# A decoder trunk on one core: sums copied into a second PSUM bank so that later matmuls accumulate onto the copy

## The chip, the core and the metric

The kernel runs on one core of one Trainium2 chip. The metric is the device time of one execution in microseconds (us); lower is better. TensorE (PE in the profile) multiplies, ScalarE (ACT) and VectorE (DVE) read its results out of PSUM, GpSimd (POOL) adds weights in SBUF, and SyncE's queue (SP) issues most of the transfers.

## The reference, cut to what matters

```python
def reference(x, ...):                       # x: 1 x 1024 positions x 1024 channels, fp32
    h = x
    for layer in range(2):
        y = _rms_norm(h, mix_norm_g[layer])
        if layer == 0: y = _chunk_gating_mixer(y, ...)       # u * (W_s v + b), then w_out
        else:          y = _dilated_attention_mixer(y, ...)  # 3 groups, dilation 1, 4, 16
        h = h + y
        y = _rms_norm(h, mlp_norm_g[layer])
        h = h + jnp.square(jax.nn.relu(y @ w_up[layer])) @ w_down[layer]   # 1024 -> 4096 -> 1024
    return _rms_norm(h, final_norm_g)
```

The attention projects q, k and v (3 groups of 8 heads of 64 channels each), adds to the scores a bias looked up in a table of 32 buckets, and merges the groups by their softmax denominators.

## The kernel before

**Split numbers.** Every fp32 factor is split into a high part that the matmul unit takes exactly (type fp32r) and a low rest: ACT makes the high part with a copy, DVE the rest with a subtraction. The helper `split` (profile lines L211 and L212) records both, so these two lines stand for all splits of the program and a reader goes by the tile: `wp` and `whi` are weights, `hx` hidden values of the MLP, `tr` other operands. A product of two factors is three matmuls (high x high, high x low, low x high), all recorded at L183.

**Seven products.** Up projection, down projection and q/k projections use Strassen's scheme in Winograd's form. A tile of 256 x 1024 outputs is made of seven products in place of eight; each product is 128 x 512 outputs over four blocks of 128 inputs, so 4 x 3 = 12 matmuls into one PSUM bank of 128 x 512. The seven results are then summed in four ways: c11 = 1 + 2, c12 = 1 + 6 + 5 + 3, c21 = 1 + 6 + 7 + 4 and c22 = 1 + 6 + 5 + 7 (numbers are products). The banks come from two pools, named `mm` (3 banks) and `at`.

**Up projection** (loop `for q in range(2, 16)`, L785 on, in each of two layers; a "tile" below is one turn of it). Product 1 goes to a bank `a`, 5 to `d`, 6 to `b`, 7 to `e`, and then 2, 3 and 4 accumulate in `a`, `d` and `e`. ACT copies `a` to `u` and `d` to `c22` (L796, L808); DVE makes five additions of 128 x 512: `u += b` (L819), `c22 += e` (L826), `c22 += u` (L834), `c12 = u + d` (L845) and `c21 = u + e` (L850). ReLU and squaring follow on ACT (L733, L734). `hidden_terms` forms the differences that the down projection needs and stores them as `hid`.

**Weights of a tile** are loaded one tile ahead (`r`), summed by POOL (L354 to L359) and split in the order of a generator, `Weights.steps`, which `more()` pumps once after each product. In layer 0, `coming_late` meanwhile loads weights of layer 1 (`t<-in_w_up`), splits them (`tr`) and stores them (`wlup`); three of its steps follow each tile. `late` loads them back.

**Down projection** (`Down`): products into `mm` and `at` banks, `b` and `h` updated by DVE (L940, L952, L921). While it ends, `begin_attention` issues the loads and splits of the first value weights.

**Attention.** `unit_qk` makes q and k of one pair of heads in one group, as seven products again: one ACT copy (L1208) and five DVE additions (`total`, L1200), then q and k are split with a strided order (`halves`, L1194 and L1195). The next unit's products are interleaved on PE with scores (L1268 on DVE, exponentials L1270 on ACT), transposes (L190) and value products of the unit before. `prepare` makes the q/k weights of coming units ahead of time (list `PREPARED`); its additions are L485 and its loads `r<-in_w_qkv`. `bias_rows` looks the bias table `tab` up by three fp32 matmuls with one-hot rows.

**What sets the order.** Each engine runs its own queue in order. The queues follow the order of the code, except that instructions under `tc.high_priority(offset=PRIO)` move up to 60 places ahead, and that side work comes from generators which are advanced by an estimated PE clock (`flow`, with the paces in `PACE` and `LAT`). `tc.issue_after(x)` puts what is in it behind x.

## Time and profile before

| | before |
|---|---|
| time, median of 3 runs | 2146.59 us (2145.32 to 2150.58) |
| the profiled execution's own time | 2148.0 us |
| its span in the profile | 2146.3 us (1.7 us lie around it) |
| granted TensorE clock, mean | 0.996 |
| PE busy / DVE / ACT / POOL | 2111.2 / 1629.2 / 1116.2 / 521.4 us |
| matmuls | 10192 |

A row of a timeline gives start, duration, engine, line, operation, what is written from what, and in brackets how long the engine had been idle before it and what it waited for. A row of groups gives busy time and mean nanoseconds of one. Matmul rows end later than the next one starts, since matmuls are pipelined: the distance of their starts is what counts.

### The profile page before, as it was taken

The numbers are of one execution on the slowest core, as the hardware profiler recorded it, in microseconds if no ns is written. First come the engines' busy times: TensorE is split into PE (matmuls) and PEld (weight loads), VectorE is DVE, ScalarE is ACT, GpSimd is POOL, SyncE is SP. The second block draws the span as 40 slices with busy tenths as digits, with TensorE's granted clock in tenths as the row PEclk, the third lists the DMA queues.
The fourth block names the chain that finished last, engine by engine and source line by source line (L and its number), as shares of the span: only waits on it lengthen the run. The fifth ranks groups of instructions, "written<-read, shape, count | busy, mean of one in ns | idle before, by whom it ended". The sixth has DMA issues, their size and how long they took to land.

```text
span 2146.3 us, 30685 instructions
## 1 busy us (share of the span) xinstructions
PE 2111.2 (98%) x10192; PEld 1740.0 (81%) x10192; DVE 1629.2 (76%) x2998; ACT 1116.2 (52%) x2258; POOL 521.4 (24%) x381
## 2 busy tenths in 40 slices
PE   9999999999999999999999999999999999999997
PEld 7888887888888888788877788877788888788886
DVE  7877678777889777788367777768876667987776
ACT  7645446555564444345256665655555556544432
POOL 2000124333333332420200000001433332432244
PEclk9999999999999999999999999999999999999999
DMA  6326814566655443449797646481154443654432
GB/s 217 124 75 217 275 69 164 172 214 213 217 184 169 162 157 119 132 161 335 268 288 219 175 153 186 162 275 69 57 198 151 152 162 121 204 168 143 143 108 79
DMA packets 214962, 367.68 MB, mean 171 GB/s; under 512 B 38809, under 2 KB 66580, under 8 KB 214804
## 3 DMA queue, kind: packets, MB, share of 16 engines
q1 hardware_dynamic: 205664, 364.37, 51.2%
q10 hardware_dynamic: 9140, 1.36, 0.4%
q8 instruction: 80, 1.31, 0.2%
q14 instruction: 78, 0.64, 0.1%
HBM read 239.13 MB, written 126.52 MB: 170 GB/s over the span
## 4 chain that ended last, share of the span: by engine, by line
PE 80%; DVE 10%; ACT 4%; DMA 4%; issue 2%; SPq 0%; POOL 0%; ACTq 0%; DVEq 0%; POOLq 0%
PE at L183 43%; PE mm L183 36%; PE at L190 1%; DVE tr L212 1%; DVE h L311 1%; DMA r<-in_w_v 1%; DMA V<-vd 1%; DVE h L921 1%; DVE y L212 1%; DVE wp L212 1%; ACT t L1270 1%; DVE N L1309 1%; DMA wd<-tr 1%; DVE t L1437 0%; ACT q L1194 0%
## 5 line engine op out<-in xcount | busy, mean ns | idle before, releaser
L211 ACT ACTIVATE wp<-r 128x512 fp32r<-128x512 f32 (+2 forms) x411 | 244.0, 597 | 346.1 <-PE at L183 222.0
L183 PE MATMUL at<-hx,wp 128*128 128x512 f32 x1740 | 406.3, 389 | 2.2 <-DVE h L921 2.0
L183 PEld LDWEIGHTS at<-hx,wp 128*128 128x128 f32 x1740 | 326.3, 188 | 71.6 <-DVE h L921 2.8
L212 DVE TENSOR_TENSOR wp<-r,wp 128x512 fp32r<-128x512 f32 (+2 forms) x404 | 308.9, 770 | 67.9 <-ACT wp L211 64.5
L183 PE MATMUL mm<-y,wp 128*128 128x512 f32 x1344 | 338.9, 395 | 1.9 <-issue 1.1
L183 PE MATMUL at<-t,wp 128*128 128x512 f32 x1344 | 313.7, 389 | 0.0
L183 PEld LDWEIGHTS at<-t,wp 128*128 128x128 f32 x1344 | 252.3, 188 | 52.4
L183 PEld LDWEIGHTS mm<-y,wp 128*128 128x128 f32 x1344 | 248.4, 188 | 54.5 <-issue 2.2
L267 POOL TENSOR_TENSOR t<-t 128x512 f32<-128x512 f32 (+1 forms) x64 | 81.6, 1275 | 703.6 <-ACT t L262 546.8
L354 POOL TENSOR_TENSOR t<-r 128x512 f32<-128x512 f32 (+3 forms) x62 | 88.7, 1431 | 582.5 <-DMA r<-in_w_dn 275.9
L183 PE MATMUL mm<-hx,wp 128*128 128x512 f32 x696 | 169.6, 390 | 0.7 <-DVE hx L212 0.3
L183 PE MATMUL mm<-y,whi 128*128 128x512 f32 x512 | 158.3, 390 | 0.0
L212 DVE TENSOR_TENSOR hx<-t,hx 128x512 fp32r<-128x512 f32 x192 | 148.7, 782 | 11.6 <-ACT hx L211 11.5
L183 PEld LDWEIGHTS mm<-hx,wp 128*128 128x128 f32 x696 | 130.2, 188 | 29.6 <-issue 1.0
L183 PE MATMUL mm<-t,wp 128*128 128x512 f32 x576 | 154.1, 403 | 0.0
L211 ACT ACTIVATE hx<-t 128x512 fp32r<-128x512 f32 x192 | 118.7, 627 | 44.2 <-DMA t<-hid 39.3
L921 DVE TENSOR_TENSOR h<-h,at 128x512 f32<-128x512 f32 x144 | 98.0, 681 | 54.6 <-PE at L183 53.9
L183 PEld LDWEIGHTS mm<-t,wp 128*128 128x128 f32 x576 | 102.6, 188 | 21.4
L183 PE MATMUL at<-y,wp 128*128 128x512 f32 x480 | 118.7, 390 | 0.0
L183 PEld LDWEIGHTS mm<-y,whi 128*128 128x128 f32 x512 | 95.6, 188 | 19.5
L1270 ACT ACTIVATE t<-t,st 128x128 f32<-128x128 f32 (+1 forms) x192 | 84.4, 441 | 50.7 <-DVE st L1268 49.4
L183 PEld LDWEIGHTS at<-y,wp 128*128 128x128 f32 x480 | 89.9, 188 | 19.9 <-issue 1.3
(214 smaller groups left out, 3531.9 us busy)
## 6 DMA issues: line engine op xcount, KB each, us to landing
t<-hid SPq DMA_DIRECT2D x182, 256.0 KB, 4.6
wd<-tr SPq DMA_DIRECT2D x154, 256.0 KB, 3.2
wp<-wd SPq DMA_DIRECT2D x77, 512.0 KB, 4.6
hid<-t SPq DMA_DIRECT2D x140, 256.0 KB, 2.7
r<-in_w_up SPq DMA_DIRECT2D x120, 256.0 KB, 2.7
r<-in_w_dn SPq DMA_DIRECT2D x80, 256.0 KB, 2.6
hid<-b SPq DMA_DIRECT2D x56, 256.0 KB, 2.9
r<-in_w_v SPq DMA_DIRECT2D x48, 256.0 KB, 3.7
```

What stands on the lines that cost most here:

```text
L183: nc.tensor.matmul(out, lhsT, rhs, **kw)
L190: nc.tensor.transpose(out, src, ident)
L211: nc.scalar.activation(hi, src, AF.Copy)
L212: (engine or nc.vector).tensor_tensor(lo, src, hi.bitcast(F32), op=ALU.subtract)
L267: nc.gpsimd.tensor_tensor(self.acc, self.acc, sq, op=ALU.add)
L311: nc.vector.tensor_tensor(x, x, ps, op=ALU.add)
L354: tt(r3, r[0, 0], r[1, 0], op=ALU.subtract)
L921: return engine.tensor_tensor(hs[i, s], hs[i, s], src, op=ALU.add).ins
L1270: nc.scalar.activation(p[:, c], p[:, c], AF.Exp, bias=m, scale=-1.0, accum_out=dn)
L1309: nc.vector.tensor_tensor(o, o, pv[r, c], op=ALU.add)
```

## The change

For tiles q = 5 to 15 of the up projection, ACT copies product 1 from its bank into a second bank `sums`, and products 6, 7 and 4 accumulate there. Between them ACT copies 1 + 6 out to `c12`, and DVE adds 1 + 6 + 7 to `c22`; the bank ends as c21. Two DVE additions are left (`c22 += sums`, L885; `c12 += d`, L891). The products run in the order 1, 5, 6, 2, 7, 3, 4, as against 1, 5, 6, 7, 2, 3, 4. The old form stays for q = 2 to 4 as `opening`. `unit_qk` is changed in the same way: three ACT copies, two additions, the last half of k straight from the bank, and the order 1, 5, 6, 2, 7, 3, 4 in place of 1, 6, 5, 2, 7, 3, 4.

Further edits: the order in which a tile's weights are split; `coming_late` takes its steps after the second, fourth and sixth call of `more` within a tile; the value weights are issued behind the last product-4 addition of the down projection; `prepare` waits at least 8000 ns of the estimated clock after its loads where these go to `raw` buffers (the last list of `PREPARED`); `bias_rows` uses two fp32r matmuls on a split table in place of one fp32 matmul; layer 1's first weights come back in another order.

```diff
@@ Weights.steps
-            for p, src in ((5, r[1, 0]), (7, r3), (6, r[1, 1]), (2, r[0, 1]), (3, r[0, 0])):
+            for p, src in ((5, r[1, 0]), (6, r[1, 1]), (2, r[0, 1]), (7, r3), (3, r[0, 0])):
@@ prepare
-            yield pace
+            yield max(pace, 8000.0) if own is raw else pace
@@ mlp, up projection
+            def more():
+                forward()
+                calls[0] += 1
+                if layer == 0 and q >= OPEN and calls[0] in LATER:
                     next(coming_late, None)
...
+            if q < OPEN:
+                c11, c21, c12, c22 = opening(q, w, more)
+            else:
+                a = at_bank()
+                product(a, w[1], x.t[1])
+                more()
+                sums = mm_bank()
+                with tc.high_priority(offset=PRIO):
+                    nc.scalar.activation(sums, a, AF.Copy)
...
+                d = at_bank()
+                product(d, w[5], x.t[5])
+                more()
+                c22 = temp()
+                nc.scalar.activation(c22, d, AF.Copy)
...
+                product(sums, w[6], x.t[6], True)
+                more()
+                c12 = temp()
+                with tc.high_priority(offset=PRIO):
+                    nc.scalar.activation(c12, sums, AF.Copy)
...
+                product(a, w[2], x.t[2], True)
+                more()
+                c11 = temp()
+                squared(c11, a)
+                product(sums, w[7], x.t[7], True)
+                more()
+                nc.vector.tensor_tensor(c22, c22, sums, op=ALU.add)
+                squared(c22)
...
+                product(d, w[3], x.t[3], True)
+                more()
+                nc.vector.tensor_tensor(c12, c12, d, op=ALU.add)
+                squared(c12)
+                product(sums, w[4], x.t[4], True)
+                c21 = temp()
+                squared(c21, sums)
@@ bias_rows
+            oh = rtemp()
+            nc.scalar.activation(oh[0:33, 0:VEC], raw[0:33, 0:VEC], AF.Copy)
             ps = at_bank()
-            matmul(ps[0:8, 0:VEC], tab[:, 8 * g:8 * g + 8], oh[0:33, 0:VEC], passes=4, start=True, stop=True)
+            for e, t in enumerate(tabs):
+                matmul(ps[0:8, 0:VEC], t[:, 8 * g:8 * g + 8], oh[0:33, 0:VEC], start=e == 0, stop=e == 1)
@@ begin_attention
-            firsts.extend(value_weights(0))
+            with tc.issue_after(emptied):
+                firsts.extend(value_weights(0))
@@ unit_qk
-        c = temp()
-        with tc.high_priority(offset=PRIO):
-            nc.scalar.activation(c, a, AF.Copy)
-        b = mm_bank()
-        product(b, w[6], x[6])
-        more()
-        total(c, b, c)
+        sums = copied(mm_bank(), a)
         d = mm_bank()
         product(d, w[5], x[5])
         more()
-        k1 = total(c, d)
+        k1 = copied(temp(), d)
+        product(sums, w[6], x[6], True)
+        more()
+        q1 = copied(temp(), sums)
         product(a, w[2], x[2], True)
...
-        halves(1, 1, own(total(k1, e, k1), g))
+        halves(1, 1, own(total(k1, sums, k1), g))
         product(d, w[3], x[3], True)
         more()
-        halves(0, 1, own(total(c, d), g))
-        product(e, w[4], x[4], True)
+        halves(0, 1, own(total(q1, d, q1), g))
+        product(sums, w[4], x[4], True)
         more()
-        halves(1, 0, own(total(c, e), g))
+        halves(1, 0, own(sums, g))
@@ before layer 1's up projection
+    first, order = [{}, {}], [(q, i, j) for j in range(2) for q in range(2) for i in range(2)]
+    for q, i, j in order[:6]:
+        first[q][i, j] = late("up", q, i, j)
```

Three places show how the queues move. The first is ACT's queue in layer 0's up projection at the start of tile q = 7, before: `mm_4531` is product 1, `at_4550` product 5, `t_4486` a layer-1 weight that `coming_late` loaded.

```order
L211 ACTIVATE wp_4544<-r_4520 128x512 [waits DMAHW3_49,PE_49]
L211 ACTIVATE tr_4488<-t_4486 128x512 [waits DMAHW7_49]
L796 ACTIVATE t_4548<-mm_4531 128x512 [waits DMAHW6_49]
L808 ACTIVATE t_4566<-at_4550 128x512 [waits PE_49]
L211 ACTIVATE wp_4563<-r_4516 128x512 [waits Pool_49]
```

The same place after the change: `at_4531` is product 1, `mm_4550` the bank of the sums, `at_4552` product 5, `t_4548` the layer-1 weight.

```order
L862 ACTIVATE mm_4550<-at_4531 128x512 [waits PE_49]
L213 ACTIVATE wp_4544<-r_4520 128x512 [waits DMAHW0_49]
L213 ACTIVATE wp_4565<-r_4516 128x512 [waits PE_49,Pool_49]
L869 ACTIVATE t_4568<-at_4552 128x512 [waits DMAHW3_49]
L213 ACTIVATE tr_4585<-t_4548 128x512 [waits DMAHW4_49,DMAHW3_49]
L876 ACTIVATE t_4591<-mm_4550 128x512 [waits PE_49]
```

The layer-1 split moved from ahead of the copy of product 1 to ahead of the copy of 1 + 6; in the next tile it stands ahead of the copy of product 1 again.

The second is DVE's queue where layer 0's down projection ends, before: `wp_87..` are the first value weights, `b_6192` and `h_92` to `h_97` sums of the down projection.

```order
L921 TENSOR_TENSOR h_92<-h_92,at_8525 128x512 [waits PE_49]
L212 TENSOR_TENSOR wp_8774<-r_8775,wp_8774 128x512 [waits DMAHW6_49,Activation_49]
L921 TENSOR_TENSOR h_96<-h_96,at_8536 128x512 [waits PE_49]
L212 TENSOR_TENSOR wp_8779<-r_8780,wp_8779 128x512 [waits DMAHW7_49,Activation_49]
L940 TENSOR_TENSOR b_6192<-b_6192,mm_8598 128x512 [waits PE_49]
```

After, the same additions and the first of the value weights (`wp_8731`, `wp_8736`):

```order
L981 TENSOR_TENSOR b_6174<-b_6174,mm_8580 128x512 [waits PE_49]
L962 TENSOR_TENSOR h_97<-h_97,at_8588 128x512 [waits PE_49]
L962 TENSOR_TENSOR h_97<-h_97,at_8596 128x512 [waits DVE_49,PE_49]
L993 TENSOR_TENSOR b_6174<-b_6174,at_8604 128x512 [waits PE_49]
L962 TENSOR_TENSOR h_93<-h_93,mm_8580 128x512 [waits PE_49]
L962 TENSOR_TENSOR h_93<-h_93,at_8588 128x512 [waits PE_49]
L962 TENSOR_TENSOR h_97<-h_97,at_8596 128x512 [waits PE_49]
L214 TENSOR_TENSOR wp_8731<-r_8732,wp_8731 128x512 [waits DMAHW1_49,Activation_49]
L214 TENSOR_TENSOR wp_8736<-r_8737,wp_8736 128x512 [waits DMAHW2_49,Activation_49]
```

All eight value-weight splits now stand behind the down projection's last additions.

The third is DVE's queue in the attention, at the second unit of the last `PREPARED` list, before: `r_10672` is a q/k weight under preparation, `st2_10636` row maxima of a group of scores.

```order
L212 TENSOR_TENSOR tr_10633<-at_10628,tr_10632 128x384 [waits Activation_49]
L485 TENSOR_TENSOR r_10672<-r_10672,r_10676 128x512 [waits DMAHW2_49]
L1268 ISA t_10657,st2_10636<-at_10643,b_10185 128x128 [waits DMAHW4_49,PE_49]
L1268 ISA st2_10636 128x1
```

After, where `r_10705` is that weight and `t_10665`, `t_10670` are scores of the same unit's second group:

```order
L1317 ISA t_10665,st2_10604<-at_10651,b_10166 128x128 [waits PE_49]
L1317 ISA st2_10604 128x1
L1317 ISA t_10665,st2_10604<-at_10651,b_10166 128x128
L1317 ISA st2_10604 128x1
L1317 ISA t_10670,st2_10604<-at_10652,b_10166 128x128 [waits PE_49]
L1317 ISA st2_10604 128x1
L1317 ISA t_10670,st2_10604<-at_10652,b_10166 128x128
L1317 ISA st2_10604 128x1
L1358 TENSOR_TENSOR N_10396<-N_10396,at_10681 64x256 [waits Activation_49]
L487 TENSOR_TENSOR r_10705<-r_10705,r_10709 128x512 [waits DMAHW6_49,DMAHW2_49]
```

The addition of the weight moved behind both groups of scores that it stood ahead of.

More of the change, by code (lines that the diff above doesn't have):

```diff
@@ L107 @@
 MMB = 3
+OPEN = 5
+LATER = (2, 4, 6)
 CALM = (1600.0, 1600.0, 1200.0, 1600.0)
@@ L373, in plain @@
             for i in range(2):
-                w[i, j] = late("up", q, i, j) if layer else wpair().split(load(w_up[layer, q, i, j]))
+                w[i, j] = wpair().split(load(w_up[layer, q, i, j]))
         return w
@@ L784, in mlp, with opening @@
         x.rest()
-        for q in range(2, 16):
-            down = Down(layer) if q == 15 else None
-            wn = down.weights(0) if down else up_weights(q + 1)
-            more = ahead(wn)
-            more()
+        def opening(q, w, more):
             a = mm_bank()
@@ L800, in mlp @@
                     more()
-            if down:
-                down.take(14, held, SEVEN[:4])
             d = at_bank()
@@ L812, in mlp @@
                     more()
-            if down:
-                down.take(14, held, SEVEN[4:])
             b = at_bank()
@@ L819, in mlp @@
             nc.vector.tensor_tensor(u, u, b, op=ALU.add)
-            if down:
-                down.early(SEVEN[:4])
             e = at_bank()
@@ L835, in mlp @@
             squared(c22)
-            if down:
-                down.early(SEVEN[4:])
             product(a, w[2], x.t[2], True)
@@ L847, in mlp @@
             product(e, w[4], x.t[4], True)
-            more()
             c21 = temp()
@@ L851, in mlp @@
             squared(c21)
-            if layer == 0 and q > 3:
-                for _ in range(3):
-                    next(coming_late, None)
+            return c11, c21, c12, c22
+        for q in range(2, 16):
+            down = Down(layer) if q == 15 else None
+            wn = down.weights(0) if down else up_weights(q + 1)
+            forward, calls = ahead(wn), [0]
+            def more():
+                forward()
+                calls[0] += 1
+                if layer == 0 and q >= OPEN and calls[0] in LATER:
+                    next(coming_late, None)
+            more()
[8 more added lines that the diff above has]
+                    nc.scalar.activation(sums, a, AF.Copy)
+                if down:
+                    down.take(14, held, SEVEN[:4])
+                d = at_bank()
[3 more added lines that the diff above has]
+                nc.scalar.activation(c22, d, AF.Copy)
+                if down:
+                    down.take(14, held, SEVEN[4:])
+                product(sums, w[6], x.t[6], True)
[3 more added lines that the diff above has]
+                    nc.scalar.activation(c12, sums, AF.Copy)
+                if down:
+                    down.early(SEVEN[:4])
+                product(a, w[2], x.t[2], True)
[6 more added lines that the diff above has]
+                squared(c22)
+                if down:
+                    down.early(SEVEN[4:])
+                product(d, w[3], x.t[3], True)
[5 more added lines that the diff above has]
+                squared(c21, sums)
@@ L855, in mlp @@
             if q < 14:
-                hidden_terms(q, c11, c21, c12, c22, u)
+                hidden_terms(q, c11, c21, c12, c22, temp())
             elif q == 14:
-                held = hidden_terms(q, c11, c21, c12, c22, u, False)
+                held = hidden_terms(q, c11, c21, c12, c22, temp(), False)
             else:
@@ L960, in run @@
                 product(e, w[4], xs(4), True)
-                then(add(1, 0, e), 4)
+                self.emptied = add(1, 0, e)
+                then(self.emptied, 4)
                 if t >= 14:
@@ L987, in close @@
                     sq.add(o)
-                after(sq)
+                after(sq, self.emptied)
     tab = small.tile([33, 24], F32, name="tab", bufs=1)
@@ L992, in trunk @@
     nc.scalar.dma_start(tab[0:32, :], rel)
+    tabs = [small.tile([33, 24], F32R, name=f"tab{e}", bufs=1) for e in range(2)]
+    split(*tabs, tab)
     bvec = dram.tile([8, 3, VEC], F32, name="bvec", bufs=1)
@@ L996, in bias_rows @@
         for g in range(3):
-            oh = temp()
-            nc.scalar.dma_start(oh[0:33, 0:VEC], onehot[:, g, :])
+            raw = temp()
+            nc.scalar.dma_start(raw[0:33, 0:VEC], onehot[:, g, :])
             yield 12000
+            oh = rtemp()
+            nc.scalar.activation(oh[0:33, 0:VEC], raw[0:33, 0:VEC], AF.Copy)
             ps = at_bank()
-            matmul(ps[0:8, 0:VEC], tab[:, 8 * g:8 * g + 8], oh[0:33, 0:VEC], passes=4, start=True, stop=True)
+            for e, t in enumerate(tabs):
+                matmul(ps[0:8, 0:VEC], t[:, 8 * g:8 * g + 8], oh[0:33, 0:VEC], start=e == 0, stop=e == 1)
             bv = temp()
@@ L1012, in trunk, with begin_attention @@
     hd = [[dram.tile([P, HALF], F32, name=f"hd{m}_{s}", bufs=1) for s in range(2)] for m in range(KT)]
-    def begin_attention(sq):
+    def begin_attention(sq, emptied):
         s = sq.cols.start // HALF
         if s == 0:
-            firsts.extend(value_weights(0))
+            with tc.issue_after(emptied):
+                firsts.extend(value_weights(0))
         flow.add((terms_a.second_plain if s else terms_a.first)(sq, 2), LAT["sum"])
@@ L1082, in unit_weights @@
             if (i, 1) in wd:
-                for p in (1, 6, 5, 2, 7, 3, 4):
+                for p in (1, 5, 6, 2, 7, 3, 4):
                     t = wpool.tile([P, 2, HALF], F32R, tag="w", name="wp")
@@ L1201, in total, with copied @@
             return t
+        def copied(out, src):
+            with tc.high_priority(offset=PRIO):
+                nc.scalar.activation(out, src, AF.Copy)
+            return out
         a = mm_bank()
@@ L1205, in unit_qk @@
         more()
-        c = temp()
-        with tc.high_priority(offset=PRIO):
-            nc.scalar.activation(c, a, AF.Copy)
-        b = mm_bank()
-        product(b, w[6], x[6])
-        more()
-        total(c, b, c)
+        sums = copied(mm_bank(), a)
         d = mm_bank()
@@ L1215, in unit_qk @@
         more()
-        k1 = total(c, d)
+        k1 = copied(temp(), d)
+        product(sums, w[6], x[6], True)
+        more()
+        q1 = copied(temp(), sums)
         product(a, w[2], x[2], True)
@@ L1219, in unit_qk @@
         halves(0, 0, own(a, g))
-        e = mm_bank()
-        product(e, w[7], x[7])
+        product(sums, w[7], x[7], True)
         more()
@@ L1553, in trunk @@
         pass
-    first = [plain(1, 0)]
+    first, order = [{}, {}], [(q, i, j) for j in range(2) for q in range(2) for i in range(2)]
+    for q, i, j in order[:6]:
+        first[q][i, j] = late("up", q, i, j)
     flow.until(lambda: (3, 1) in outs)
@@ L1558, in trunk @@
     start_terms(sq[1], 1, 3, terms)
-    first.append(plain(1, 1))
+    for q, i, j in order[6:]:
+        first[q][i, j] = late("up", q, i, j)
     quarter = lambda i: slice(i * 256, (i + 1) * 256)
@@ L1575, in final, with finish @@
             yield LAT["out"]
-    def finish(sq):
+    def finish(sq, emptied):
         flow.add(final(sq), LAT["sum"])
```

## The prediction

> **What bounds the kernel now.** The page comes first: the busy times, and the engines' shares of the chain that ended last.

> ```profile
> PE 2111.2 (98%) x10192; PEld 1740.0 (81%) x10192; DVE 1629.2 (76%) x2998; ACT 1116.2 (52%) x2258; POOL 521.4 (24%) x381
> ...
> PE 80%; DVE 10%; ACT 4%; DMA 4%; issue 2%; SPq 0%; POOL 0%; ACTq 0%; DVEq 0%; POOLq 0%
> ```

> PE is busy for 2111.2 of 2146.3 us, so 35.1 us are all that can be won without taking matmuls away. The next view asks where these 35 us lie: busy times by stretch, in the order PE, PEld, DVE, ACT, POOL, then granted clock and DMA share. The stretches are the two up projections and the attention.

> ```profile
> 345.00:610.00 265.00, 265.00 (x1171) 219.42 (x1170) 206.96 (x260) 155.07 (x270) 88.55 (x59) 1.00 0.59 201
> 1540.00:1820.00 280.00, 280.00 (x1237) 231.86 (x1236) 202.80 (x259) 156.58 (x275) 95.14 (x63) 1.00 0.44 150
> 1075.00:1420.00 345.00, 336.51 (x2096) 275.06 (x2095) 250.13 (x754) 210.41 (x598) 0.00 (x0) 1.00 0.67 199
> ```

> In both up projections PE has no gap at all (265.00 of 265.00, 280.00 of 280.00): the additions that the change takes away cost PE nothing there. In the attention PE is idle for 8.5 us. A piece of the chain of waits shows one tile: start, length, what.

> ```profile
> 409.00 8.16 PE at L183 x36
> 417.16 2.72 PE mm L183 x12
> 419.88 5.44 PE at L183 x24
> 425.32 2.72 PE mm L183 x12
> ```

> From 409.00 to 428.04 (425.32 + 2.72) is 19.04 us for seven products, 2.72 us each, or 0.2267 us for one matmul. That is what the matmuls alone take.

> **Part 1, the up projection (q = 5 to 15, 22 tiles).** Three DVE additions and no matmul go.

> ```profile
> L826 DVE TENSOR_TENSOR t<-t,at 128x512 f32<-128x512 f32 x28 | 19.2, 685 | 21.7 <-PE at L183 21.6
> ...
> L1200 DVE TENSOR_TENSOR t<-t,mm 128x512 f32<-128x512 f32 x60 | 40.7, 683 | 13.3 <-PE mm L183 12.7
> ```

> That is 22 x 3 x 0.685 = 45 us of DVE, from a stage in which nobody waits for DVE: worth 0. In exchange `sums` is written, read and written again by turns. Three times a tile a handoff must end within one product, 2.72 us: the copy into the bank while 5 runs, the copy of 1 + 6 while 2 runs, the addition of 1 + 6 + 7 while 3 runs. The nearest rows are the PSUM-to-SBUF copy (0.58 us, below) and the addition (0.685); a copy from PSUM to PSUM is in no row. Between half and twice 0.58 it fits, and I take 0.58. So 2.72 - 0.69 leaves 2.0 us in which the copy or addition may still be held up in its queue. The three value 0 if held up for less, and the excess each time if for more.

> [...]

> **Part 2, the last up tile.** At q = 15 the down projection's loads of hidden values (`hr`) are split on ACT. In the changed queue two such splits stand directly ahead of the copy of 1 + 6, which PE awaits 10.88 us (four products) after the tile starts. Rows of PE and ACT, layer 0:

> ```profile
> 596.52 2.88 PE L183 MATMUL mm<-y,wp 128*128 128x512 f32 x12
> ```

> ```profile
> 606.06 1.27 ACT L211 ACTIVATE hx<-hr 128x512 fp32r<-128x512 f32 x2 [0.88 <-DMA hr<-hid]
> ```

> The tile starts at 596.52; the splits end at 607.33, 10.8 us in. With the copy behind them (0.58) PE waits about 0.5 us. Bounds: 0 if the load lands 0.5 us sooner, 1.2 if it is as much later. Layer 1 has no such wait in its rows; I take +0.5 in all.

> **Part 3, the bias table.** Rows of PE:

> ```profile
> 329.47 0.81 PE L183 MATMUL at<-t,tab 33*8 33x384 f32 x2
> 330.21 1.66 PE L183 MATMUL mm<-y,wp 128*128 128x512 f32 x6
> ```

> One fp32 matmul takes 330.21 - 329.47 = 0.74 us of PE. Two fp32r ones take 2 x 384/512 x 0.2267 = 0.34. Three groups: -1.2 us (between -1.0 and -1.3). The additional copies and split of the table (33 partitions, off PE's path) cost 0.

> **Part 4, value weights behind the down projection.** DVE and PE, before:

> ```profile
> 898.99 1.60 DVE L212 TENSOR_TENSOR wp<-r,wp 128x512 fp32r<-128x512 f32 x1 [0.74 <-ACT wp L211]
> 900.52 0.68 DVE L940 TENSOR_TENSOR b<-b,mm 128x512 f32<-128x512 f32 x1
> ```

> ```profile
> 901.25 1.67 PE L183 MATMUL mm<-hx,y 128*128 128x512 f32 x6 [1.51 <-DVE b L940]
> ```

> L940 frees a bank, and ran late because a value-weight split ahead of it waited for ACT and then took 1.60 us. After the change all eight stand behind the last additions: the 1.51 us go. The same eight splits (about 0.68 each) then fall into the value projection, whose additions leave DVE room; late weights there could give back up to 1, from the 1.60 that one took here. I take -1.4 (-0.5 to -1.5).

> **Part 5, layer 1's first weights.**

> ```profile
> 1504.01 0.94 PE L183 MATMUL mm<-y,wp 128*128 128x512 f32 x3 [1.15 <-issue]
> ```

> ```profile
> L519 SPq DMA_DIRECT2D wp<-wlup x8: 319/320/320, 1483.4 to 1502.9; - x8
> ```

> Eight weights are loaded up to 1502.9, each as a buffer comes free, and the matmul at 1504.01 waits 1.15 us. The two it needs were fifth and sixth in SP's queue; the new order makes them third and fourth. -1.15 (-0.6 to -1.2); next late would be the fifth, which PE needs a stage later.

> **Part 6, the pace of the last prepared weights.** DVE, then PE:

> ```profile
> 1124.23 0.69 DVE L485 TENSOR_TENSOR r<-r 128x512 f32<-128x512 f32 x1 [5.93 <-DMA r<-in_w_qkv]
> 1124.83 0.28 DVE L1268 CUSTOM_DVE_ANT_0 t<-at,b 128x128 f32<-128x128 f32 x1
> ```

> ```profile
> 1125.71 1.49 PE L190 MATMUL at<-ident,t 128*128 128x128 f32 x4 [2.38 <-ACT t L1270]
> ```

> DVE sat 5.93 us on a load with the scores queued behind, so exponentials and transposes came late and PE idled 2.38 us, its longest wait for the attention. The changed order puts the addition behind both groups of scores: -2.2 (-0.5 if the load then holds up the splits of the transposes instead, -2.4 if nothing is left).

> **Part 7, q and k.** Per unit, three of five additions go and two copies come. Rows of the waits of PE, and of the groups that split k:

> ```profile
> PE at L183 <- DVE k L1195: 1.7, 4, 0.8
> ```

> ```profile
> L1194 ACT ACTIVATE k<-t 128x512 fp32r<-128x512 f32 x24 | 23.0, 956 | 15.1 <-DVE t L1200 15.1
> ...
> L1195 DVE SCALAR_TENSOR_TENSOR k<-t,k 128x512 fp32r<-128x512 f32 x24 | 23.6, 983 | 6.8 <-ACT k L1194 6.7
> ```

> Four times PE waited for the last half of k, 1.7 us in all, 0.8 at the longest. That half now comes straight from the bank: the 0.683 us of addition and its handoff drop from the chain, which covers the three short ones (on average (1.7 - 0.8) / 3 = 0.3) and most of the longest: -1.3 (-0.5 to -1.7). Against it, the bank of the sums is now read by ACT (0.96) and DVE (0.98) and, where units follow at once, the next product that takes that bank is one product away: 1.94 and two handoffs against 2.72. An example is the `t,wp` product at 1182.23 here, which starts while k is still being split:

> ```profile
> 1182.23 0.86 PE L183 MATMUL mm<-t,wp 128*128 128x512 f32 x3
> ...
> 1184.25 0.85 PE L183 MATMUL at<-k,q 64*128 64x128 f32 x10 [0.75 <-DVE k L1195]
> ```

> I take +0.3, between 0 and 1.5. The weights' new split order moves 7 behind 6 and 2 and leaves every split well ahead of its product; in the down projection, where products keep their order, I take 0 (-0.5 to +1.5).

> **The sum.** -1.2 - 1.4 - 1.15 - 2.2 - 1.3 + 0.5 + 0.3 = -6.45 us. On the profiled execution's 2148.0 us that is 2141.6; against the median of the runs, 2146.59, it is 2140.1. All low ends together give -3.1 + 4.2 = +1.1, all high ends -8.6.

> **The rivals.** A difference of 0.3% (6.4 us) is about what a measurement of this kernel can tell from no change, and the forecast lies right at that line.

> *Waits come back elsewhere.* In a queue that runs in order, a wait that goes often uncovers the next. If parts 4, 6 and 7 give half (-2.5) and the losses are doubled (+1.6), the sum is -2.35 - 2.5 + 1.6 = -3.2, time 2143.4. For it: the attention's stalls are many and small, and the load behind the 5.93 us is still needed. Against: parts 3 and 5 hang on nothing of this.

> *A handoff on the sums is held up, slower.* Layer 0 interleaves loads and splits of layer-1 weights. ACT, before:

> ```profile
> 432.28 0.63 ACT L211 ACTIVATE tr<-t 128x512 fp32r<-128x512 f32 x1 [2.75 <-DMA t<-in_w_up]
> 432.82 0.58 ACT L796 ACTIVATE t<-mm 128x512 f32<-128x512 f32 x1
> ```

> Product 1 ended at 428.04; its copy began at 432.82, 4.78 us later, since the split ahead of it waited for a load. Before, that was harmless. After, a copy that begins 4.78 us late ends at 5.36 and PE waits 5.36 - 2.72 = 2.64 us. [...] In the changed order such a split stands ahead of one of the two copies in nearly every layer-0 tile. If five loads land as late as this one, 5 x 2.64 = 13.2 us are lost: 2140.1 + 13.2 = 2153.3. It decides from the point at which the load lands more than 2 us after the product's end. Against it: the loads are now issued earlier within the tile, one ahead of the third weight load, a product or more before the split. I give it 0.11.

> *More goes than I counted.* If the DVE time set free shortens PE's other small waits too, such as

> ```profile
> PE at L183 <- DVE h L921: 2.0, 2, 1.0
> ```

> and every high end holds, -8.6 - 2.0 = -10.6: 2136.0.

> **How the numbers follow.** Forecast 0.46 (2138 to 2143), waits come back 0.33, handoff held up 0.11, more goes 0.10. Faster by over 0.3% (below 2140.2): 0.6 of the forecast's case, since its two losses may as well be nothing, 0.3 of the next, and all of the last: 0.28 + 0.10 + 0.10 = 0.48. Slower by over 0.3% is the handoff's case but for its mildest form, 0.10. The rest, 0.42, is within 0.3%. The range holds the forecast, the case of returning waits with its low ends, and most of the case in which more goes: 2136 to 2147.

> **What would show it.** Right: the up projections keep PE busy without a gap, the idle times at the bias matmuls' place shrink by 0.4 each, and the waits `b L940` 1.51, `issue` 1.15 and `t L1270` 2.38 are gone from PE's list. Wrong: PE waiting for `mm L862` or `t L876` in layer 0's tiles at a spacing of 19 or 38 us, a new wait for `tr L214` in the attention just after the moved addition, or PE's idle time at 35 us as before.

## The result, and the profile after

The changed kernel takes 2162.47 us (median of 6 runs, 2160.37 to 2164.93), the kernel before 2148.65 (6 runs beside them, 2145.32 to 2151.26). The ratio is 1.0065 [1.0051, 1.0078]: 14 us slower, where 6.45 us less was forecast.

The page of after: its span, and the busy times of the engines.

```profile
span 2161.9 us, 30552 instructions
...
PE 2119.5 (98%) x10192; PEld 1747.0 (81%) x10192; DVE 1560.9 (72%) x2897; ACT 1143.8 (53%) x2308; POOL 510.7 (24%) x381
```

DVE gave up 1629.2 - 1560.9 = 68 us of work, as the change means it to, and the span is 2161.9 - 2146.3 = 15.6 us longer. PE holds the account. Its idle time rose from 35.1 to 2161.9 - 2119.5 = 42.4 us (+7.3), and its busy time rose by 2119.5 - 2111.2 = 8.3 us with the very same 10192 matmuls, so some matmuls ran slower. The first question is where the idle time lies. Waits of PE in after: engine and line waited for, us in total, times, longest.

```profile
PE at L185 <- ACT tr L1045: 6.3, 1, 6.3
PE mm L185 <- DVE h L313: 4.2, 8, 1.5
PE at L192 <- DVE tr L214: 3.1, 4, 0.9
PE at L185 <- DMA V<-vd: 3.1, 1, 3.1
...
PE at L185 <- DVE tr L214: 1.7, 4, 0.5
```

Two single waits stand out that before has not at that size. The first is new: PE waits 6.3 us for one small copy on ACT, the one-hot row of the bias table (L1045). The timeline of after around it: the load is issued, then ACT's rows up to the copy, then PE.

```profile
318.71 0.31 ACTq L1042 DMA_DIRECT2D t<-in_onehot  x1
...
333.45 0.63 ACT L213 ACTIVATE t<-b 128x512 fp32r<-128x512 f32 x1 [2.08 <-DVE b L420]
...
333.98 1.13 ACT L213 ACTIVATE t<-keep 128x512 fp32r<-128x512 f32 x2
...
335.02 0.51 ACT L1045 ACTIVATE tr<-t 33x384 fp32r<-33x384 f32 x1
...
335.58 0.81 PE L185 MATMUL at<-tr,tab 33*8 33x384 f32 x2 [6.33 <-ACT tr L1045]
336.32 2.93 PE L185 MATMUL mm<-y,wp 128*128 128x512 f32 x6
```

The row was sent for at 318.71, 16 us before ACT got to its copy. The copy itself is 0.51 us, but it stands in ACT's queue behind splits of the normalisation, and those wait for DVE (2.08 us for b, L420). PE, also in order, stands behind the matmul on that copy. Before, the matmul read the loaded row directly and started without a wait at 329.47. The last row shows the second loss: six matmuls take 2.93 us in the trace. Stretches of after (PE, PEld, DVE, ACT, POOL busy, then granted clock and DMA share):

```profile
334.00:336.00 2.00, 0.42 (x2) 0.10 (x2) 1.91 (x3) 1.53 (x4) 2.00 (x2) 0.61 0.84 273
336.00:338.00 2.00, 2.00 (x6) 1.40 (x5) 2.00 (x2) 0.00 (x0) 1.92 (x2) 0.50 0.07 27
338.00:340.00 2.00, 2.00 (x6) 1.52 (x6) 1.71 (x3) 0.63 (x1) 0.51 (x1) 0.50 0.00 0
340.00:342.00 2.00, 2.00 (x8) 1.58 (x7) 0.50 (x1) 0.52 (x1) 0.00 (x0) 0.68 0.11 32
342.00:344.00 2.00, 2.00 (x11) 1.63 (x10) 0.24 (x1) 0.63 (x1) 0.00 (x0) 1.00 0.00 0
```

After the gap the granted clock is 0.50 until about 341 us, and 6 to 8 matmuls fit into 2 us in place of 11. Loss at half clock: 2 x 0.5 + 2 x 0.5 + 2 x 0.32 = 2.6 us; with the gap, 9.0.

The second wait is the value load at 1433 us. The row of PE there, then the clock behind it (PE busy, clock, DMA share):

```profile
1433.42 1.84 PE L185 MATMUL at<-tr,V 128*128 128x128 f32 x8 [3.07 <-DMA V<-vd]
```

```profile
1435.00:1438.00 3.00, 3.00 (x15) 0.50 1.05 405
1438.00:1441.00 3.00, 3.00 (x15) 0.50 1.02 413
1441.00:1444.00 3.00, 3.00 (x9) 0.54 1.02 418
```

Before, the same matmul waited 0.58 us (1423.09), with no half clock. Here 2.5 us more of waiting and 1.5 + 1.5 + 1.4 = 4.4 us of half clock. The two places make 9.0 + 2.5 + 4.4 = 15.9 us, as much as the 15.6. So everything else, both signs together, comes to about nothing in this pair of profiles; it is not nothing one by one. Other waits went, and half clock stands at two more places in each profile: near 1142 and 1503 us in after, near 47 and 1129 in before.

### The profile page after: what moved, and what is told of

Same layout as the page of the kernel before. It is cut to its first block, busy times and chain, and to the rows that moved or that the text cites. A ratio compares the mean times of both kernels' runs of the same rounds, so it can differ in the third digit from the quotient of the medians.

```text
span 2161.9 us, 30552 instructions
## 1 busy us (share of the span) xinstructions
PE 2119.5 (98%) x10192; PEld 1747.0 (81%) x10192; DVE 1560.9 (72%) x2897; ACT 1143.8 (53%) x2308; POOL 510.7 (24%) x381
## 4 chain that ended last, share of the span: by engine, by line
PE 81%; DVE 8%; DMA 4%; ACT 3%; issue 2%; SPq 0%; POOL 0%; DVEq 0%; POOLq 0%; ACTq 0%
PE at L185 42%; PE mm L185 39%; PE at L192 1%; DMA wp<-wd 1%; DVE h L313 1%; DVE hx L214 1%; DVE t L1486 1%; DVE tr L214 1%; DVE y L214 1%; DMA h<-in_xT 0%; DVE wp L214 0%; ACT t L1319 0%; DVE N L1358 0%; DMA r<-in_w_v 0%; DVE r L415 0%
## 5 line engine op out<-in xcount | busy, mean ns | idle before, releaser
L214 DVE TENSOR_TENSOR wp<-r,wp 128x512 fp32r<-128x512 f32 (+2 forms) x404 | 323.7, 806 | 129.7 <-ACT wp L213 126.1
L185 PE MATMUL mm<-t,wp 128*128 128x512 f32 x1368 | 345.5, 396 | 1.0 <-DVE k L1243 1.0
L185 PEld LDWEIGHTS mm<-t,wp 128*128 128x128 f32 x1368 | 251.2, 188 | 55.0 <-DVE k L1243 2.1
L185 PE MATMUL at<-y,wp 128*128 128x512 f32 x1008 | 246.5, 391 | 0.0
L185 PEld LDWEIGHTS at<-y,wp 128*128 128x128 f32 x1008 | 189.9, 189 | 40.2 <-issue 0.7
L185 PE MATMUL mm<-y,wp 128*128 128x512 f32 x816 | 216.5, 405 | 1.9 <-issue 1.2
L185 PEld LDWEIGHTS mm<-y,wp 128*128 128x128 f32 x816 | 152.5, 193 | 35.2 <-issue 2.2
L214 DVE TENSOR_TENSOR hx<-t,hx 128x512 fp32r<-128x512 f32 x192 | 156.7, 820 | 3.2 <-ACT hx L213 2.9
L358 POOL TENSOR_TENSOR r<-r 128x512 f32<-128x512 f32 (+3 forms) x62 | 90.9, 1466 | 181.4 <-DVE wp L214 162.5
L185 PE MATMUL at<-t,wp 128*128 128x512 f32 x552 | 130.6, 389 | 0.0
L185 PEld LDWEIGHTS at<-t,wp 128*128 128x128 f32 x552 | 103.6, 188 | 21.5
```

What stands on the lines that cost most here:

```text
L185: nc.tensor.matmul(out, lhsT, rhs, **kw)
L214: (engine or nc.vector).tensor_tensor(lo, src, hi.bitcast(F32), op=ALU.subtract)
L358: tt(r[1, 1], r[1, 0], r[0, 0], op=ALU.subtract)
```

## The experiments

The theory (A): the copy's place in ACT's queue makes most of the loss, the q/k products a little, the rest is neutral. Rivals: the up projection's handoffs (the prediction's own slow case), a loss spread over many small waits, or the two matmuls and the copy being dear in themselves. Ratios are against the kernel before on the same chip.

### One part taken out or done alone

The changed kernel with the bias rows as before:

```diff
-            oh = rtemp()
-            nc.scalar.activation(oh[0:33, 0:VEC], raw[0:33, 0:VEC], AF.Copy)
-            for e, t in enumerate(tabs): matmul(ps, t, oh, ...)
+            matmul(ps, tab, oh, passes=4, ...)       # fp32, the row as loaded
```

> The changed kernel with one part undone: the bias rows are made by one fp32 matmul straight from the loaded one-hot rows, as before. Theory A (two new PE gaps, each longer than 3 us and each followed by matmuls at half clock: the bias copy's 6.33 us and the V load's 3.07 us): the gap at 329 us and the 0.50 clock behind it go, about 6.3 + 3.2 - 1.2 = 8.3 us, so some 2154 against the 2162.5 of the changed kernel; the gap at V<-vd stays near 3 us. Rival B (the accumulation onto a copy itself costs PE time, spread over the up and q/k products, and the bias gap would otherwise show as a wait a little later): 2160 to 2163.

Measured: 2155.3 us, ratio 1.0017 [1.0006, 1.0028]. The gap at the bias matmul is gone and so is its half clock.

The kernel before with the bias rows of the change (the same lines the other way round):

> The kernel before with the bias rows' edit alone (two fp32r matmuls on a split table, one-hot rows copied by ACT). Theory A: the second copy stands in ACT's queue behind the same normalisation splits as in the changed kernel, PE waits some 6 us at the second bias matmul and runs at half clock for 6 us after: 2148.7 + 8.3 = 2157. Rival B, and the prediction's part 3: 2147.5.

Measured: 2159.75 us, ratio 1.0045 [1.0029, 1.0061]. PE of this kernel:

```profile
335.92 0.81 PE L183 MATMUL at<-tr,tab 33*8 33x384 f32 x2 [6.35 <-ACT tr L1003]
```

The same gap to 0.02 us, with nothing else of the change in the program. So the bias rows cost 0.45 per cent alone and 0.48 by taking them out (1.0065 - 1.0017), about 10 us.

The kernel before with the q/k part alone (`sums = copied(mm_bank(), a)`, products 6, 7, 4 onto it, last half of k from the bank):

> The kernel before with the q/k form alone (copy into a second bank, order 1, 5, 6, 2, 7, 3, 4). Theory A: in SP's queue the load of the exchanged statistics now stands ahead of the last V loads and holds them up; PE waits about 3 us for V near 1425 us and then runs at half clock for 8 us: 2148.7 + 6.8 = 2155, with the four waits for k turned into waits of 0.5. The prediction's part 7: 2147.7, no wait for V beyond 0.6. Rival B: 2152 without any wait over 1.5 us.

Measured: 2153.7 us, ratio 1.0013 [1.0000, 1.0026], an interval that starts at no change. The wait for V that theory A puts at 3 us is 1.38; the loss stands elsewhere. Its timeline at one of two new waits, ACT and DVE splitting k out of the bank, PE behind them:

```profile
1148.03 0.60 ACT L1194 ACTIVATE k<-mm 128x512 fp32r<-128x512 f32 x1
...
1149.06 0.63 DVE L1195 SCALAR_TENSOR_TENSOR k<-mm,k 128x512 fp32r<-128x512 f32 x1
...
1149.75 1.05 PE L183 MATMUL mm<-t,wp 128*128 128x512 f32 x3 [2.53 <-DVE k L1195]
```

The last half of k is read from the bank (`k<-mm`) by two engines one after the other, each in its own queue, and the next unit's product needs that bank. Among the waits of PE it comes twice:

```profile
PE mm L183 <- DVE k L1195: 3.8, 2, 2.5
```

The kernel before with the up projection's part alone, and with the side orders alone (late loads, pace, issue order of the value weights):

```diff
+ up projection of the change                      (first kernel)
+ late("up", ...), max(pace, 8000.0), issue_after(emptied)   (second kernel)
```

> The kernel before with the up projection's new form alone (copy into a second bank, split order, spread steps of the layer-1 weights). Theory A and the prediction's part 1: no PE gap in either up projection, 2148.7 within 1.5 us. Rival B: 5 us or more slower, PE busy time of the up stages longer than 19.04 us a tile.

> The kernel before with three of the smaller edits and nothing else: order of layer 1's first weights, pace of 8000 for the last prepared weights, value weights behind the down projection. The prediction's parts 4, 5 and 6: -1.4 - 1.15 - 2.2 = -4.75 us, 2145.4 against 2150.1. From the changed kernel's trace: the 1.15 stays (PE waits there for something else than the loads), the 1.51 at L940 goes but 1.5 to 2 us come back in the value projection, the 2.38 goes: about -2 us, 2148.

Measured: 0.9997 [0.9986, 1.0009] (2150.22 us) and 0.9999 [0.9987, 1.0010] (2151.19 us). Neither can be told from no change, and the -4.75 us of parts 4 to 6 lies outside the second interval (-2.8 to +2.2 us). In the second the two waits that it aims at (1.51 and 2.38) are gone, but a row of PE shows what came in their place:

```profile
1131.96 1.14 PE L183 MATMUL at<-tr,V 128*128 128x128 f32 x7 [2.55 <-DVE tr L212]
```

The four ratios multiply to 1.0045 x 1.0013 x 0.9997 x 0.9999 = 1.0054, inside the interval of the whole change.

Up projection and side orders together, q/k and bias rows as before:

> The kernel before with the up projection's part of the change and the late loads, pace and issue orders, without the q/k products and the bias rows of the change. Theory A (the loss sits in the bias rows and the q/k products; the rest is neutral, since waits that go come back): ratio 0.998 to 1.001 against the kernel before, no gap over 3 us that the kernel before lacks. Rival C (up projection and side orders help each other, or hurt each other): below 0.997 or above 1.002.

Measured: 2150.79 us, ratio 1.0003 [0.9994, 1.0012]. No gain from their being together, no loss.

### Is it the copy's place?

The changed kernel with PE kept busy in the gap by matmuls that nobody reads:

```diff
+            if g == 1:
+                for _ in range(24):
+                    nc.tensor.matmul(ps[:, 0:P], ones, ones, start=True, stop=True)
```

> The changed kernel with 24 idle fp32 matmuls of 128x128 (about 0.2 us each, results thrown away) put on PE in the gap ahead of the second bias matmul; the ACT copy that PE waits for stays where it is. It leaves the wait and takes away only the idleness. Theory A (idle time of 6.33 us costs itself, and another 3.2 us by matmuls at half clock after it): the granted clock stays 1.00 behind the gap and the time falls by about 3 us, 2159.5 against 2162.5. Rival C (the half clock has another cause than the idle gap): time unchanged, 0.50 clock still behind the place.

Measured: 2163.49 us, ratio 1.0061 [1.0043, 1.0079]. Stretches of this kernel:

```profile
336.00:338.00 2.00, 1.90 (x8) 1.33 (x9) 2.00 (x3) 0.04 (x1) 1.92 (x2) 1.00 0.35 126
338.00:340.00 2.00, 2.00 (x10) 1.66 (x9) 1.60 (x1) 0.30 (x1) 1.05 (x1) 1.00 0.00 0
```

With PE busy the clock stays at 1.00, so at this place the half clock follows from the idle time. From the bias matmul to the fifth group of six matmuls behind it, PE takes 342.11 - 336.10 = 6.01 us here and 344.20 - 335.58 = 8.62 in after: 2.6 us are won at the place itself. They do not show in the total, 1.0061 against 1.0065; the two intervals are wider than 3 us (0.0014), and the profiled execution, the longest of its six, lost time elsewhere (4.52 us on the value load).

The copy half way to its matmul (and the `ex` load behind the value loads, which the next section takes up):

```diff
-            yield 12000
+            yield 6000
             oh = rtemp()
             nc.scalar.activation(oh[0:33, 0:VEC], raw[0:33, 0:VEC], AF.Copy)
+            yield 6000
```

> The changed kernel with both waits mended and every edit kept: the one-hot copy is issued half way between its load and its matmul (it stood at the end), and the exchange load stands behind the V loads as in e6. Theory A: no gap over 2 us, bias matmuls shorter than before: about 1 us under e6, 2150. Rival: the ACT copy finds another queue place with a wait, PE idle 1 to 3 us there, 2153.

Measured: 2158.42 us, ratio 1.0032 [1.0020, 1.0045]. Timeline of this kernel, ACT's work ahead of the copy, the copy, ACT's next work, and PE:

```profile
327.19 0.63 ACT L213 ACTIVATE t<-b 128x512 fp32r<-128x512 f32 x1 [1.67 <-DVE b L420]
...
328.91 0.63 ACT L213 ACTIVATE y<-r 128x512 fp32r<-128x512 f32 x1 [1.09 <-DVE r L415]
329.44 0.51 ACT L1045 ACTIVATE tr<-t 33x384 fp32r<-33x384 f32 x1
329.86 1.53 ACT L735 ACTIVATE t<-mm 128x512 f32<-128x512 f32 x3
...
330.48 2.50 PE L185 MATMUL mm<-y,wp 128*128 128x512 f32 x6 [4.19 <-ACT t L735]
```

The copy no longer makes its own matmul wait. Now ReLU copies of the up projection (L735) stand behind it and behind splits that wait 1.67 and 1.09 us for DVE; in after they were done by 327.73, ahead of these splits. PE idles 4.19 us for one of them, before the copy's matmul. The gap moved with the copy, though the copy itself is only 0.51 us of it.

The copy on GpSimd:

```diff
-            nc.scalar.activation(oh[0:33, 0:VEC], raw[0:33, 0:VEC], AF.Copy)
+            nc.gpsimd.tensor_copy(oh[0:33, 0:VEC], raw[0:33, 0:VEC])
```

> The changed kernel with one line altered: the copy of the one-hot row stands on GpSimd instead of ScalarE. Theory A (the cost of the bias edit is the copy's place behind some twenty normalisation splits in ScalarE's queue): GpSimd is idle at that point, the 6.3 us gap at the table's first matmul goes, no half-clock stretch follows, and the time falls by about what the old bias rows gave, 7 to 10 us, to a ratio of 1.001 to 1.003. Rival B (any copy between the load and the matmul costs, or the two matmuls instead of one): the gap stays over 3 us and the ratio stays above 1.005.

Measured: 2164.43 us, ratio 1.0078 [1.0064, 1.0092]. The expectation missed. Timeline of this kernel:

```profile
333.84 1.59 POOL L422 TENSOR_TENSOR keep<-keep,b 128x512 f32<-128x512 f32 x1 [1.90 <-DVE b L420]
...
335.81 1.28 POOL L356 TENSOR_TENSOR t<-r 128x512 f32<-128x512 f32 x1 [0.39 <-DMA hid<-t]
...
337.05 0.96 POOL L1045 CAST tr<-t 33x384 fp32r<-33x384 f32 x1
...
338.06 0.81 PE L185 MATMUL at<-tr,tab 33*8 33x384 f32 x2 [8.99 <-POOL tr L1045]
```

GpSimd was not idle there: it waits for the same DVE addition (b, L420) and then has weights to add, the copy takes 0.96 us in place of 0.51, and the gap became 8.99 us.

The copy some 24 us ahead, beside the first group's, into a buffer of its own:

```diff
+    ohs = [small.tile([33, VEC], F32R, name="oh1", bufs=1)]
+    src = temp()
+    nc.scalar.dma_start(src[0:33, 0:VEC], onehot[:, 1, :])
+    nc.scalar.activation(ohs[0], src[0:33, 0:VEC], AF.Copy)
...
+            if g != 1: (as changed)
+            else: oh = ohs[0]
```

> The changed kernel with the second group's one-hot row loaded and copied once, ahead of the whole row loop, into a buffer of its own: the copy lands in ScalarE's queue just ahead of the first group's, near 305 us, and not behind the splits near 335. Theory A (queue place alone): no wait of the table's second matmul, no half-clock stretch at 336 to 342, and the time falls to that of the variant with the old bias rows or 0.8 us below, ratio 1.001 to 1.003. Rival B (the two matmuls and their table splits cost in themselves): the ratio stays at 1.004 or above though the gap is gone.

Measured: 2155.32 us, ratio 1.0021 [1.0011, 1.0031], that of the old bias rows. Its timeline:

```profile
305.24 0.51 ACT L1040 ACTIVATE oh<-t 33x384 fp32r<-33x384 f32 x1
...
329.30 0.51 PE L185 MATMUL at<-oh,tab 33*8 33x384 f32 x2
329.74 1.66 PE L185 MATMUL mm<-y,wp 128*128 128x512 f32 x6
```

Copy and two matmuls are all still there, no wait and no half clock follow, and the pair takes 329.74 - 329.30 = 0.44 us of PE where the fp32 matmul took 0.74. That settles it for the bias rows: the loss is the copy's place in a queue, not the copy or the matmuls.

### The value load, and the bank of the sums

In the queue of SP the q/k part puts the load `ex<-sc` ahead of the value loads; before, it stood behind them. The changed kernel with old bias rows and that load behind the value loads:

```diff
+        with tc.issue_after(U[NU - 2].last_V) if (u.hp, g) == (3, 1) else nullcontext():
             nc.sync.dma_start(e, sc)
```

> e1 (old bias rows) with one load moved in SP's queue: the last load of the exchanged statistics for dilation 4 is issued behind the last V loads. Theory A: the wait for V (2.3 us in e1, 3.07 us with half clock behind it in the changed kernel) shrinks to 0.6 or less, as before, and the slow executions at a clock of 0.992 become rare: about 2151, 4 us under e1. Rival D (V is late because the 16 DMA engines are full, wherever it stands in SP's queue): wait still 2 us, time as e1, 2155.

Measured: 2153.84 us, ratio 1.0012 [0.9999, 1.0026], against 1.0017 without the reorder. The wait for V is 1.71 us where it was 2.33. Within the noise: the order matters little.

Both kernels unchanged, profiled a second time:

> The kernel before, unchanged, profiled a second time. If the value load's wait belongs to the kernel, it is 0.4 to 0.8 us again; if it varies from one execution to the next (DMA engines full in both), it may be anything from 0 to 3 us here too. At the bias table's second matmul there is no wait in either case.

> The changed kernel, unchanged, profiled a second time. The wait at the bias table's second matmul is a matter of order and comes again, 6.0 to 6.6 us, with some 6 us at half clock behind it. The value load's wait: 2.7 to 3.5 us again with half clock behind it if it belongs to the kernel, elsewhere between 1 and 5 us, with or without half clock, if it varies by execution.

PE in the second profile of after:

```profile
335.38 0.80 PE L185 MATMUL at<-tr,tab 33*8 33x384 f32 x2 [6.34 <-ACT tr L1045]
```

```profile
1435.50 1.94 PE L185 MATMUL at<-tr,V 128*128 128x128 f32 x8 [5.53 <-DMA V<-vd]
```

The bias gap came again to 0.01 us. The value load's wait did not: 3.07 and 5.53 us in after, 0.58 and none in before. It is no fixed cost: with the DMA engines full (a share of 1.22 from 1420 to 1423 in before, 1.08 from 1432 to 1435 in after), it changes from one execution to the next. In the kernels with the q/k part of the change it was 1.38 to 5.53 us (0.70 in the variant below); without that part, nothing to 2.61 (2.61 in the up-and-side kernel, where the queue has the old order). What makes it so much longer in after than with the old bias rows (3.07 and 5.53 against 2.33) stays open; it is long in two more kernels that lose time at the bias rows (4.52 with the filled gap, 4.43 with the copy on GpSimd), but 0.18 in the bias rows alone.

In the second profile of before, the waits that parts 4 and 6 aim at are 0.29 and 3.20 us, where the first had 1.51 and 2.38. So what part 4 was to win comes and goes as well.

The q/k part alone, with the bank of the sums from the other pool:

```diff
-        sums = copied(mm_bank(), a)
+        sums = copied(at_bank(), a)
```

> The kernel before with the q/k part of the change alone, and the bank of the sums taken from the other PSUM pool (five banks, shared with the attention) instead of the pool of three that the products use. Theory A (in the q/k part alone, products of the next unit wait 1.3 and 2.5 us because the last half of k is split straight from a bank that a pool of three has to hand on): the two waits for k L1195 in front of a product of the unit's weights go, 3.8 us to under 1, and the ratio falls from 1.0013 to 0.999 to 1.001. Rival F (the wait moves to the attention's banks, which then come free later): waits of transposes or of products with V for k L1195 or for a bank, of 2 us or more in all, and the ratio stays at 1.001 or above.

Measured: 2174.69 us, ratio 1.0113 [1.0100, 1.0127]. The result of this variant is not the reference's (relative error 0.095); no run shows why (last section), and only its waits are read. Waits of PE:

```profile
PE at L183 <- DVE tr L212: 12.3, 10, 2.2
```

No wait for k is left, as expected, and the attention pays: 12.3 us for transposes' splits against 1.9 in the q/k part alone. The rival holds: by this variant, a bank that is kept through four products is dearer in the pool that the attention turns over.

### A version that beats both

Up projection and side orders of the change, the early copy of the bias rows, q/k products as before:

> The same early copy, with the up projection and the late loads, pace and issue orders of the change, but the q/k products as before. Theory A (q/k products cost 0.1 to 0.2 per cent, the up projection and the orders nothing, the bias rows give back 0.8 us once the copy stands early): ratio 0.9985 to 1.0005. Rival C (something in the bias rows still costs, wherever the copy stands): 1.002 or above.

Measured: 2148.19 us (2146.28 to 2150.79), against 2151.20 for the kernel before beside it; ratio 0.9989 [0.9981, 0.9998]. The interval just excludes no change: some 2 us gained, and by the two ratios (1.0065 - 0.9989 of 2150 us) 16 us better than the change as it was made.

This kernel and the one with the copy far ahead differ in the q/k part alone and ran beside the same kernel before: 2148.19 against 2155.32 us, with intervals that do not meet. Here the q/k part costs 7 us, where alone it cost about 3. It is no small item, and its price depends on what stands around it.

## Why the prediction was wrong

**Part 3 failed, and it is the largest miss.** "The additional copies and split of the table (33 partitions, off PE's path) cost 0." The price of the work was nearly right (0.51 us a copy; 0.44 us against 0.74 for the matmuls, where 0.34 was worked out). What was not asked is where the copy stands in ACT's queue: behind splits that wait for DVE, while PE's queue has the matmul at its fixed place. A gain of 1.2 was booked; the runs showed a loss of 10 us (1.0045 alone, 1.0017 without it). The prediction had seen what a queue in order does, in its rival of the up projection (a copy 4.78 us late behind a split that waited for a load), and it reckoned with that in parts 4 and 6, but not here. In the up projection it did not cost PE anything: no wait for the copies L862 or L876 is among PE's, and stretches of after in both up projections show PE without a gap.

```profile
345.00:610.00 265.00, 265.00 (x1170) 218.99 (x1169) 169.90 (x221) 157.74 (x275) 79.12 (x59) 1.00 0.56 192
1550.00:1830.00 280.00, 279.99 (x1235) 231.52 (x1234) 169.87 (x226) 161.61 (x284) 86.91 (x64) 1.00 0.44 151
```

**Part 1 was right:** 0. The copy from bank to bank, in no row before, took 0.58 us as assumed. DVE's share there fell from 206.96 to 169.90 us of 265 and bought nothing. The copies and the addition on the sums ended within the product of 2.72 us that each had: PE is busy for 265.00 of 265 us. **Part 2** was on the small side of its range: no wait at q = 15, where +0.5 was taken.

**Parts 4, 6 and 7: the waits went and others came.** Part 4, like the description of the change, took it that all eight value weights stand behind the down projection's last additions. They do not: its closing part (the last hidden blocks, `xe`) still adds to h, and splits of value weights stand between these additions. Rows of DVE and PE in after:

```profile
922.39 1.82 DVE L214 TENSOR_TENSOR wp<-r,wp 128x512 fp32r<-128x512 f32 x1 [0.72 <-ACT wp L213]
...
924.13 1.87 DVE L313 TENSOR_TENSOR h<-h,mm 128x512 f32<-128x512 f32 x3
...
924.86 2.35 PE L185 MATMUL mm<-xe,we 128*128 128x512 f32 x9 [1.51 <-DVE h L313]
```

The 1.51 of part 4 came back here in full, by the mechanism that part 4 describes and ahead of the value projection, the only place where it looked for a return. In the side orders alone it did not come back.

Part 6's wait of 2.38 gave way to one of 1.29. DVE still stands on the same load, for 6.58 us, and PE's matmul starts 0.6 us after the addition that waited for it has ended:

```profile
1137.73 0.69 DVE L487 TENSOR_TENSOR r<-r 128x512 f32<-128x512 f32 x1 [6.58 <-DMA r<-in_w_qkv]
```

```profile
1138.98 1.66 PE L185 MATMUL at<-tr,V 128*128 128x128 f32 x8 [1.29 <-issue]
```

In the side orders alone it is the one of 2.55 for the transposes' splits, behind 4.97 us on that load. Part 6 named this as its low end, still a gain of 0.5; there it took the whole.

Part 7's four waits of scores for k are gone, and four of up to 0.50 for the transposes' splits stand in the list, 1.7 us in all as before. Its loss was mis-sized: the bank read by two engines, booked at +0.3 (0 to 1.5), measured 3.8 us in the q/k part alone. In the changed kernel it is 1.0:

```profile
1121.31 0.96 PE L185 MATMUL mm<-t,wp 128*128 128x512 f32 x3 [1.01 <-DVE k L1243]
```

So "waits come back elsewhere" is what happened to these parts. With its own price that case gave 2143.4; without the bias rows the change measured 1.0017, some 4 us slower than before.

**Part 5 read the wrong releaser.** The wait of 1.15 us on "issue" is still there:

```profile
1520.66 0.94 PE L185 MATMUL mm<-y,wp 128*128 128x512 f32 x3 [1.16 <-issue]
```

The 1502.9 that part 5 reads as the end of the loading is when the eighth load was issued. The fourth to sixth, with the two that it needs, were issued from 1494.83 on:

```profile
1494.83 1.68 SPq L519 DMA_DIRECT2D wp<-wlup  x3
```

The longest of these loads took 3.5 us to land, so both weights were there by 1500, 4 us ahead of the matmul. In after they are third and fourth in the queue, and the wait is as long as before (1.15). So it is not for those loads; "issue" means that the profile shows no releaser, and the prediction put a load there by guess. In both profiles the matmul starts 0.1 us after an addition to h has ended on DVE (L311, in after L313), which frees a bank; that this is what it waits for is not shown.

**The clock was in no term.** Half clock after the gap made 2.6 of the 9.0 us at the bias rows, and more at the value load. Before showed it already, behind the 2.38 us that part 6 priced by themselves:

```profile
1128.00:1130.00 2.00, 2.00 (x10) 1.17 (x8) 1.06 (x2) 1.26 (x4) 0.00 (x0) 0.50 0.69 150
```

**How the miss adds up.** Between the forecast of -6.45 us and the measured +14 lie some 20. By the ratios of the parts taken alone, part 3 makes about 11 of them (-1.2 forecast, +9.7 measured), parts 4 to 6 about 5 (-4.75, and nothing to be told from zero), and part 7 about 4 (-1.0, and +2.8). So the sign does not hang on part 3 alone: without the bias rows the change is still slower, 1.0017 [1.0006, 1.0028].

## What to carry to other kernels

Price an added instruction by its place, not its length: for each one on an in-order queue, read what stands ahead of it there, what that waits for, and which engine's queue is blocked until it is done. An operation that PE must wait for belongs as far ahead as its inputs allow, beside work that is itself on time; here no wait was left some 24 us ahead, half way was not enough (4.19 us of PE idle), and another engine that waits for the same addition was worse (8.99 us). And work taken from an engine that nobody waits for (45 us of DVE in the up projection) bought nothing: 0.9997 [0.9986, 1.0009].

## What the runs showed of the hardware

```profile
1142.00:1145.00 3.00, 3.00 (x15) 2.50 (x14) 2.48 (x7) 2.21 (x8) 0.00 (x0) 0.50 0.31 119
```

```profile
1426.00:1429.00 3.00, 3.00 (x28) 2.59 (x28) 1.66 (x4) 1.64 (x5) 0.00 (x0) 1.00 1.03 375
```

The first line is that of after, the second that of up-and-side. So half clock stood behind waits from 1.29 us on, and not behind one of 2.61; what decides it is not shown.

Nor does it take a wait. At 1498.93 in after, PE runs 24 matmuls of one column each, with no wait listed since one of 0.23 us at 1494.27; behind them the clock stands at 0.50 from 1502 to 1505, and the next 15 matmuls take 5.28 us where they take 3.69 in before.

What half clock cost came in portions of about 1.7 us. The time lost, (1 - clock) summed over stretches of 1 us, is 1.70 and 1.71 us in before (near 47 and 1129) and 3.41, 3.41, 5.12 and 1.70 us in after (near 338, 1143, 1438 and 1503), the program's end left out: about 3.4 us of half clock, or twice or three times as long. In the kernel with the copy on GpSimd, in wider stretches, it is 5.12 (332 to 344) and 1.71 (1434 to 1440). A longer wait need not cost more: the sum is 3.41 at the 6.33 us, part of it while PE still waited, and 5.12 at the 3.07.

Accumulation onto a copy that ACT wrote gave the reference's result with the copy in the pool of three banks (the q/k part alone, 1.0013), and a relative error of 0.095 with it in the pool `at` (the variant of 1.0113). The banks of `at` also take narrower results (of 1 and 128 columns among them), but no run here took these away: the cause is not shown.
